# One core, one hybrid decoder layer: a hand-written order from the mixer's output projection to the first gate products of the MLP, split weights kept in DRAM, and 114-row transfers cut in two

## The chip, the core and the metric

The kernel runs on one core of a Trainium2 chip. The metric is the time on the device, in microseconds, of one execution; a kernel is run several times and the median counts. In what follows PE is TensorE (PEld its weight loads), ACT is ScalarE, DVE is VectorE, POOL is GpSimd and SP is SyncE, whose queue issues most of the DMAs.

## The reference

All data are float32; the layer is computed once (depth 1, batch 1, 1024 tokens of 1024 features, 16 learned tokens ahead of them).

```python
u = rmsnorm(h, mix_norm_pre[l])
q, f_logit, i_in, g_out, v_pool, gate_a, gate_b = jnp.split(u @ w_in[l], cuts, axis=-1)
a = hgrn2(q, f_logit, i_in, g_out, lbs[l], hgrn_out_norm[l])      # 4 heads, chunked recurrence
p = multiscale_pool(v_pool, pool_proj[l], pool_scale[l])          # trailing means, 4 groups
z = sigmoid(gate_a) * (a @ w_branch_hgrn[l]) + sigmoid(gate_b) * (p @ w_branch_pool[l])
h = h + rmsnorm(z @ w_out[l], mix_norm_post[l])
u = rmsnorm(h, ffn_norm_pre[l])
gt = causal_dwconv(u @ ffn_w_gate[l], ffn_conv_w[l], ffn_conv_b[l])     # 1024 -> 2816, width 3
y = (gelu(gt) * (u @ ffn_w_up[l])) @ ffn_w_down[l]
h = h + rmsnorm(y, ffn_norm_post[l])
```

The change concerns the sixth to the eighth of these lines: `z @ w_out`, the residual and the two norms, and the first products of `u @ ffn_w_gate`.

## The kernel before, in words

**Precision.** Every large product is made from three: both operands are split into a first part rounded to the matmul's format (`hi`, an ACT copy) and the rest (`lo`, a subtraction on DVE or POOL), and hi x hi, hi x lo and lo x hi are added up in PSUM (`mm3`, L158). For weights `wsplit` (L131) does this: a DMA on SP into `wraw` (three buffers), the ACT copy into `whi`, the subtraction into `wlo` (three buffers each). A `Loader` (L140) holds three weight blocks ahead: `ahead()` splits the block that comes three places later.

**The mixer's output.** 1026 tokens count here (the last two learned ones are kept for the convolution). They are taken in three thirds of 342 (`c`), each of three row tiles of 114 rows (`i`, RT = 114). `mix_mm` (L1055) runs over the eight feature blocks `k` of `w_out`; for each it takes the 128 x 1024 weight block, split in `whi` and `wlo`, and for each row tile and each half of the columns three matmuls: 18 per block, 144 per third, 432 in all. The split of `z` for a block (`split_z`, L935: an ACT copy, a DVE subtraction) is made four blocks ahead. The same 24 (c, k) weight blocks are loaded and split anew for each third; the subtraction runs on POOL, but for the last two blocks, which have it on DVE (L997).

**Behind each third.** `mix_out` (L1077) makes, for each row tile and half, the sum of squares (ACT) and the product with the gain into `m1` (DVE) out of PSUM. `vec` (L1090) takes the residual row (`load_res`, L1000, a load of 114 rows), finishes the norm, adds the residual, stores the sum `hs` to DRAM for the end of the kernel (L1096, a store of 114 rows), and norms the sum again into `un`. `feat` (L1099) transposes `un` on PE (L1017, eight transposes into one pair of PSUM banks) and fills the operands of the MLP, `to_quarters` (L1012). For a third, these steps are placed between the blocks of the next one (`reorder`, L1107, and the list at L1118).

**The MLP's products.** The gate and up projections use a Strassen scheme of seven products per pair of 128-column blocks (class `Strassen`, L180). Its moving operands are quarters of the activations: b11 and b21 are the two feature halves of the first 514 tokens, b22 the second feature half of the others, and t1 to t4 sums of quarters, which need all tokens. So P1 (b11) and P2 (b21) of the first four gate units can run before the last rows are normed: eight products of 24 matmuls. P6 (t2), P5 (t1), P3 (b22), P7 (t3) and P4 (t4) of the first unit follow. For a row tile behind token 512 `to_quarters` copies the transposes (ACT, `tt`), makes t1, t2, t3 and their hi and lo parts (DVE and ACT), the lo part of b22 and the difference for t4 (POOL); its last step, the parts of t4, is returned as a function (`t4s`) for later. `load_unit` (L220) loads a unit's weights and makes four weight sums on POOL. `ahead` (L199) of this class splits the weights of coming products, two products to a buffer, on DVE, but for products 5 to 8 of the early ones, which go to POOL (L210).

**What sets the order.** In most of the kernel a scheduler orders each engine's instructions by its own estimate, starting from program order; inside `tc.manual_schedule(engines=...)` the named engines keep program order. Before the change that holds for the start of the kernel and for POOL in the MLP (L1280), not for the mixer's output. SP is left to the scheduler in both kernels, and its queue issues in order: an issue that waits for a buffer holds back those behind it. Row tiles, z parts, `m1`, `un`, residual rows, t quarters and sums share 24 slots of SBUF (`slot`, L88); PSUM is four pairs of banks here (`pair`, L97), three of which a third of the mixer holds.

Of the kernel before, what the change touches and what calls it, by code (L numbers as in the profile page):

```python
# [8 lines left out]
F32 = mybir.dt.float32  # L9
# [47 lines left out]
def trunk_kernel(ctx: ExitStack, tc: tile.TileContext, x, meta_tokens, mix_norm_pre,  # L57
# [82 lines left out]
    class Loader:  # L140


        def __init__(self, srcs):
            self.srcs, self.got, self.at = srcs, [], 0
            self.ahead()

        def ahead(self):
            while len(self.got) < min(len(self.srcs), self.at + AHEAD):
                self.got.append(wsplit(*self.srcs[len(self.got)]))

        def next(self):
            self.at += 1
# [27 lines left out]
    class Strassen:  # L180
# [7 lines left out]
        def __init__(self, units, run, early, quarters, span, put, whole):  # L188
            self.units, self.run, self.early, self.bq = units, run, early, quarters
            self.span, self.put, self.whole = span, put, whole  # L190
            self.raws, self.sums, self.p1s, self.halves = {}, {}, {}, {}
            self.seq = []
            for e in range(0, early, 2):
                self.seq += [(e, "P1"), (e + 1, "P1"), (e, "P2"), (e + 1, "P2")]
            for u in run:
                self.seq += [(u, p) for p in self.ORDER if u >= early or p not in ("P1", "P2")]
            self.got, self.at = [], 0

        def ahead(self, n):  # L199

# [44 lines left out]
                return self.raws[u, "raw"][("P1", "P2", "P4").index(p)]  # L245
            return self.sums[u][("P5", "P6", "P7", "P3").index(p)]

        def product(self, u, p):

            assert self.seq[self.at] == (u, p)  # L250
            x = pair(p)
            self.at += 1
            whi, wlo = self.got[self.at - 1]
            q = self.MOVING[p]
            c0, o0, n = self.span(u)
            cuts = [(c0, o0, 512 - o0), (c0 + 512 - o0, 512, n - 512 + o0)][: 1 + (n + o0 > 512)]
            for k in range(4):
                xh, xl = (self.bq[q + h][k * len(self.bq[q + h]) // 4] for h in "hl")
                kk = k % xh.shape[1]
                xh, xl = xh[:, kk, :], xl[:, kk, :]  # L260
                for c, o, w in cuts:
                    pe.matmul(x[:, o : o + w], whi[:, k, :], xh[:, c : c + w], start=(k == 0), stop=False)  # L262
                    pe.matmul(x[:, o : o + w], whi[:, k, :], xl[:, c : c + w], start=False, stop=False)  # L263
                for c, o, w in cuts:
                    pe.matmul(x[:, o : o + w], wlo[:, k, :], xh[:, c : c + w], start=False, stop=(k == 3))  # L265
            self.ahead(4)
            return x[:, o0 : o0 + n]

        def half(self, key, i, n, name):

# [11 lines left out]
        def first(self, u):  # L282
            n = self.span(u)[2]
            key = (("e", u // 2), u % 2) if u < self.early else (("u", u), 0)
            self.p1s[u] = self.half(*key, n, "p1")
            return (lambda: act.copy(self.p1s[u], self.product(u, "P1")),
                    lambda: self.put(u, 0, 0, self.p1s[u], self.product(u, "P2")))

        def start_pair(self, e):
            p = [self.first(e + i) for i in range(2)]  # L290
# [697 lines left out]
    def add_quarters(*names):  # L988
        for q in names:
            for h in "hl":  # L990
# [3 lines left out]
    g3 = gain_bc(ffn_norm_pre, "g3")  # L994
    RT = CW // 3

    wo = Loader([(wblock(w_out[0], k, 1, 0, D), 1, D, dve if (c == 2 and k > 5) else pool_e)  # L997
                 for c in range(3) for k in range(KD)])

    def load_res(t0):  # L1000
        row = slot(D, name="row2")
# [1 line left out]
            nc.sync.dma_start(row[:HALO], meta_tokens[T0:NM, :])  # L1003
            nc.sync.dma_start(row[HALO:RT], x[0, 0 : RT - HALO, :])
        else:
            nc.sync.dma_start(row[:RT], x[0, t0 - HALO : t0 - HALO + RT, :])
        return row

    def t_tmp(n, name):
        return slot(n, name=nm(name))  # L1010
# [41 lines left out]
        pool_e.tensor_tensor(dst, rr(fq[q + "h"][0][:, :, d]), src, ALU.subtract)  # L1052
        pool_e.tensor_tensor(dst, rr(fq[q + "l"][0][:, :, d]), dst, ALU.add)

    def mix_mm(c, between, zs):  # L1055
        rows.update({c * CW + i * RT: load_res(c * CW + i * RT) for i in range(3)})
        banks = [pair_banks("pm") for _ in range(3)]
        znext = []
        for k in range(KD):
            whi, wlo = wo.next()  # L1060
            if k == KD - 1 and c < 2:
                znext = [split_z(c + 1, k_) for k_ in range(ZA)]
            zh, zl = zs[k]
            for i in range(3):
                t = slice(i * RT, (i + 1) * RT)
                for j in range(2):
                    n = slice(j * 512, (j + 1) * 512)
                    mm3(banks[i][j][:RT], (zh[:, t], zl[:, t]), (whi[:, 0, n], wlo[:, 0, n]), k == 0, k == KD - 1)
            wo.ahead()
            if k + ZA < KD:  # L1070
                zs.append(split_z(c, k + ZA))
            if between:
                for f in between.pop(0):
                    f()
        return banks, znext

    def mix_out(c, banks, g2, g3):  # L1077
        todo = []
        for i in range(3):
            m1 = slot(D, name="m1")  # L1080
            ssq = small([P, 2], "ssq2", "mq", 6)
            for j in range(2):
                n = slice(j * 512, (j + 1) * 512)
                junk = t_tmp(512, "junk")
                act.activation(junk[:RT], banks[i][j][:RT], AF.Square, accum_out=ssq[:RT, j : j + 1])
                dve.tensor_tensor(m1[:RT, n], banks[i][j][:RT], g2[:RT, n], ALU.mult)  # L1086
            un = {}
            t0 = c * CW + i * RT

            def vec(i=i, m1=m1, ssq=ssq, un=un, t0=t0):  # L1090
                row = rows.pop(t0)
                s = small([P, 1], "mss", "ms")
                dve.tensor_tensor(s[:RT], ssq[:RT, 0:1], ssq[:RT, 1:2], ALU.add)
                rstd = row_rstd(s, RT, "m")
                dve.scalar_tensor_tensor(m1[:RT], m1[:RT], rstd[:RT], row[:RT], ALU.mult, ALU.add)
                nc.sync.dma_start(hs[t0 : t0 + RT, :], m1[:RT])  # L1096
                un[0] = norm_rows(m1, RT, g3)

            def feat(un=un, t0=t0):  # L1099
                return to_quarters(un[0], t0, pair_banks())  # L1100

            todo += [vec, feat]
        return todo

    rows = {}

    def reorder(t):  # L1107

        v0, f0, v1, f1, v2, f2 = t
        return [[v0], [v1], [f0], [v2], [f1], [f2]]  # L1110

    between = []
    for c in range(2):
        banks, z0 = mix_mm(c, between, z0)
        between = reorder(mix_out(c, banks, g2, g3))
    v0, v1_, f0, v2_, f1, f2 = (x_[0] for x_ in between)
    t4s = []
    banks, _ = mix_mm(2, [[v0], [v1_, v2_], [f0], [lambda: add_quarters("t2", "t3", "t4"), lambda: t4s.append(f1())],  # L1118
                          [lambda: t4s.append(f2())], [lambda: [f() for f in t4s]]], z0)


    WD = ffn_w_down[0]
# [31 lines left out]
    def add_later(all_=False):  # L1154
        tick[0] += 1
        for e in [e for e in later if all_ or e[0] <= tick[0]]:
            later.remove(e)
            pool_e.dma_start(e[1], e[2], accum_op=ALU.add)

    v0, f0, v1_, f1, v2_, f2 = mix_out(2, banks, g2, g3)  # L1160

    UNITS = ([(j, 0) for j in range(EARLY)] + [(j, 1) for j in range(EARLY)]
             + [(j, up) for j in range(EARLY, KF // 2) for up in range(2)])
# [97 lines left out]
        return [((yh[:, h], yl[:, h]), (wh[:, h], wl[:, h])) for h in (slice(0, 512), slice(512, 1024))]  # L1261


    ffn.begin()
    v0()
    v1_()
    v2_()
    t4s = []
    for e in range(0, EARLY, 2):
        p = ffn.start_pair(e)  # L1270
        p[0][0]()
        p[1][0]()
        t4s.append((f0 if e == 0 else f2)())
        p[0][1]()
        if e == 0:
            t4s.append(f1())
        p[1][1]()
    for f in t4s:
        f()
    with tc.manual_schedule(engines={E.Pool}):  # L1280
        ffn.finish()
        add_later(True)
# [146 lines left out]
```

## Time and profile before

| | |
|---|---|
| median of 3 runs | 1434.69 us (1431.66 to 1434.87) |
| the profiled execution's own time | 1431.93 us |
| its span, first to last instruction | 1430.1 us |
| mean granted TensorE clock | 0.979 |
| busy PE / DVE / ACT / POOL | 95% / 68% / 40% / 40% of the span |
| the mixer's output, first to last matmul | 605.6 to 728.1 us |

How to read it: the profile is one execution. Times are from the span's start. Busy shares are means over stages with different limits, so the stage from 605 to about 800 us is read by itself, in windows. An instruction that waits for a port or a lock counts as busy; matmuls overlap, and their rate is read from the distance of their starts. The granted clock is the share of the full TensorE clock. Where a row ends in `[4.33 <-DVE m L1086]`, the engine was idle for 4.33 us before the instruction and that one released it. The DMA share is the mean busy share of the core's 16 DMA engines.

### The profile page before, as it was taken

How to read it: one execution, taken by the hardware profiler on the slowest of the kernel's cores; microseconds unless marked ns; L12 is line 12 of the kernel's file. 1: busy time of each engine (PE TensorE's matmuls, PEld its weight loads, DVE VectorE, ACT ScalarE, POOL GpSimd, SP SyncE). 2: the span in 40 equal slices, each digit the busy share in tenths (PEclk: the TensorE clock that was granted, in tenths of full speed). 3: DMA queues.
4: the chain of work that ended last, by engine and by line, in shares of the span. 5: the costliest groups of instructions: out<-in, count | busy, mean ns of one | idle time of the engine just before them, and what ended most of it. 6: DMA issues, size and time to landing. Idle time of an engine off the chain costs nothing. (4 is left out here: it accounts for less than half of the span.)

```text
span 1430.1 us, 21631 instructions
## 1 busy us (share of the span) xinstructions
PE 1364.1 (95%) x8405; PEld 1233.2 (86%) x8405; DVE 976.1 (68%) x1406; ACT 570.1 (40%) x981; POOL 570.3 (40%) x400
## 2 busy tenths in 40 slices
PE   8989999999999999998968999999999999999976
PEld 6789999999999899976658888888899998888765
DVE  6784545489876754625678888888888775445476
ACT  6443333366654452244464322322222233333353
POOL 4255421237354410253348565544556642001051
PEclk9999999999999999999988999999999999999998
DMA  6034333321110033644542577666677798565546
GB/s 240 36 97 141 126 111 104 97 60 45 33 47 5 23 133 103 218 139 153 166 126 80 142 232 206 186 174 158 162 166 165 169 259 232 194 194 180 191 158 218
DMA packets 129562, 202.65 MB, mean 142 GB/s; under 512 B 7739, under 2 KB 75935, under 8 KB 129460
## 3 DMA queue, kind: packets, MB, share of 16 engines
q1 hardware_dynamic: 118548, 181.08, 37.9%
q0 software_dynamic: 10912, 20.19, 9.4%
q8 instruction: 66, 1.08, 0.3%
q14 instruction: 36, 0.29, 0.1%
HBM read 152.45 MB, written 71.85 MB: 157 GB/s over the span
## 5 line engine op out<-in xcount | busy, mean ns | idle before, releaser
L137 POOL TENSOR_TENSOR wlo<-wraw,whi 128x1024 fp32r<-128x1024 f32 (+2 forms) x37 | 85.3, 2311 | 228.2 <-ACT whi L136 146.5
L262 PE MATMUL P<-v,whi 128*128 128x258 f32 (+2 forms) x528 | 165.8, 328 | 10.9 <-DVE m L1086 4.3
L263 PE MATMUL P<-v,whi 128*128 128x258 f32 (+2 forms) x528 | 164.8, 325 | 0.7 <-POOL v L327 0.7
L265 PE MATMUL P<-v,wlo 128*128 128x258 f32 (+2 forms) x528 | 143.0, 325 | 0.0
L161 PE MATMUL pd<-rot 128*128 128x512 f32 x284 | 111.9, 394 | 8.6 <-DVE rot L1249 8.6
L262 PEld LDWEIGHTS P<-v,whi 128*128 128x128 f32 x528 | 103.1, 195 | 19.1 <-DVE m L1086 4.5
L136 ACT CAST whi<-wraw 128x1024 fp32r<-128x1024 f32 (+2 forms) x60 | 52.9, 884 | 158.6 <-PE pba L174 26.7
L162 PE MATMUL pd<-rot 128*128 128x512 f32 x284 | 111.3, 392 | 0.0
L263 PEld LDWEIGHTS P<-v,whi 128*128 128x128 f32 x528 | 103.1, 195 | 8.8 <-POOL v L327 1.0
L1249 DVE TENSOR_TENSOR rot<-yt,rot 128x1024 fp32r<-128x1024 f32 (+1 forms) x38 | 46.8, 1231 | 90.1 <-ACT rot L1248 90.1
L209 ACT CAST whi<-wraw 128x512 fp32r<-128x512 f32 x90 | 53.2, 617 | 109.6 <-PE P L263 94.4
L265 PEld LDWEIGHTS P<-v,wlo 128*128 128x128 f32 x528 | 90.0, 194 | 7.8
L1133 POOL TENSOR_TENSOR ys<-y 128x512 f32<-128x512 f32 x22 | 34.3, 1559 | 142.0 <-issue 99.4
L210 DVE TENSOR_TENSOR wlo<-wraw,whi 128x512 fp32r<-128x512 f32 x82 | 73.7, 921 | 18.2 <-ACT whi L209 18.2
L235 POOL TENSOR_TENSOR swa<-wraw,wraw 128x512 f32<-128x512 f32 x30 | 47.4, 1582 | 95.5 <-DMA wraw<-in_w_in_dram 62.3
L1248 ACT CAST rot<-yt 128x1024 fp32r<-128x1024 f32 (+1 forms) x38 | 37.7, 995 | 118.7 <-PE pd L161 118.7
L160 PE MATMUL pd<-rot 128*128 128x512 f32 x284 | 75.8, 390 | 1.2 <-ACT rot L1248 1.2
L161 PEld LDWEIGHTS pd<-rot 128*128 128x128 f32 x284 | 53.8, 190 | 21.5 <-DVE rot L1249 10.3
L209 ACT CAST whi<-swa 128x512 fp32r<-128x512 f32 x60 | 35.8, 618 | 87.8 <-PE P L263 74.9
L1183 DVE SCALAR_TENSOR_TENSOR y<-g,par,y 128x1024 f32<-128x1024 f32 x44 | 64.1, 1457 | 0.7
L160 PEld LDWEIGHTS pd<-rot 128*128 128x128 f32 x284 | 53.2, 188 | 12.7 <-ACT rot L1248 1.6
L162 PEld LDWEIGHTS pd<-rot 128*128 128x128 f32 x284 | 53.8, 190 | 11.2
(347 smaller groups left out, 4306.9 us busy)
## 6 DMA issues: line engine op xcount, KB each, us to landing
wraw<-in_w_in_dram SPq DMA_DIRECT2D x36, 512.0 KB, 3.5
yt<-ysum SPq DMA_DIRECT2D x33, 512.0 KB, 3.6
wraw<-in_ffn_w_gate_dram SPq DMA_DIRECT2D x26, 512.0 KB, 8.3
wraw<-in_w_out_dram SPq DMA_DIRECT2D x24, 512.0 KB, 8.7
wraw<-in_ffn_w_up_dram SPq DMA_DIRECT2D x22, 512.0 KB, 4.7
wsum<-in_ffn_w_down_dram SPq DMA_DIRECT2D x22, 512.0 KB, 5.9
ysum<-ys SPq DMA_DIRECT2D x11, 768.0 KB, 4.6
sa<-sscr SPq DMA_DIRECT2D x16, 513.0 KB, 5.2
```

The lines of the kernel that those rows point to most:

```text
L136: act.copy(hi, raw)
L137: eng.tensor_tensor(lo, raw, rr(hi), ALU.subtract)
L160: pe.matmul(ps, ahi, bhi, start=first, stop=False)
L161: pe.matmul(ps, ahi, blo, start=False, stop=False)
L162: pe.matmul(ps, alo, bhi, start=False, stop=last)
L209: act.copy(hi, src)
L210: (pool_e if 4 <= i < 2 * self.early else dve).tensor_tensor(lo, src, rr(hi), ALU.subtract)
L235: pool_e.tensor_tensor(s1, a21, a22, ALU.add)
L262: pe.matmul(x[:, o : o + w], whi[:, k, :], xh[:, c : c + w], start=(k == 0), stop=False)
L263: pe.matmul(x[:, o : o + w], whi[:, k, :], xl[:, c : c + w], start=False, stop=False)
L265: pe.matmul(x[:, o : o + w], wlo[:, k, :], xh[:, c : c + w], start=False, stop=(k == 3))
L1183: dve.scalar_tensor_tensor(a, g[:, :, j : j + n], cvw[:, j, m : m + 1], a, ALU.mult, ALU.add)
```

## The change

The stage from the mixer's output to the first gate products is written anew.

1. *Second parts kept.* In the first third, each `lo` part of `w_out` is also stored to DRAM by a DMA that POOL issues. In the other two thirds it is loaded from there, into the `wlo` buffer itself, instead of being subtracted again.
2. *Transfers.* The residual loads and the `hs` stores of 114 rows become one of 112 rows and one of 2.
3. *Order.* `mix_mm`, `mix_out` and `reorder` go. PE, ACT, DVE and POOL keep program order from the first matmul of the mixer's output to the last part of t4. A third's squares, gain products and adds come at its end; its norms and transposes come in the next third, the transposes behind blocks 2, 3 and 4. The last three blocks of the last third run row tile by row tile, and each tile's steps start when it is complete. Squares and gain products are one instruction per row tile of 1024 columns, no longer two of 512.
4. *Early products.* A product can have a consumer (`then`) that is placed ahead of the next weight splits, and the number of splits ahead is listed by hand (`prompt`). The transposes of the last third come after the third, fourth and sixth of the eight early products.

```diff
+    wlos = [dram.tile([P, D], F32, name=f"wlos{k}") for k in range(KD)]
+
+    def wo_parts(c, k):
+        if c == 0:
+            hi, lo = wsplit(wblock(w_out[0], k, 1, 0, D), 1, D, pool_e)
+            pool_e.dma_start(wlos[k], rr(lo[:, 0]))
+            return hi, lo
+        raw = wraw_tile()
+        nc.sync.dma_start(raw, w_out[0][k * P : (k + 1) * P])
+        hi, lo = (wst.tile([P, D], F32R, tag=t, name=nm(t)) for t in ("whi", "wlo"))
+        nc.sync.dma_start(rr(lo), wlos[k])
+        act.copy(hi, raw)
+        return [t.rearrange("p (k c) -> p k c", k=1) for t in (hi, lo)]
...
+    def by_rows(move):
+        for r in (slice(0, RT - HALO), slice(RT - HALO, RT)):
+            move(r)
...
-            nc.sync.dma_start(row[:RT], x[0, t0 - HALO : t0 - HALO + RT, :])
+            by_rows(lambda r: nc.sync.dma_start(row[r], x[0, t0 - HALO + r.start : t0 - HALO + r.stop, :]))
...
+        def take(self, i):
+            m1, ssq = slot(D, name="m1"), small([P, 1], "ssq2", "mq", 6)
+            junk = t_tmp(D, "junk")
+            act.activation(junk[:RT], self.x[i][:RT], AF.Square, accum_out=ssq[:RT])
+            dve.tensor_tensor(m1[:RT], self.x[i][:RT], g2[:RT], ALU.mult)
...
+        def add(self, i):
+            rstd = row_rstd(self.ssq[i], RT, "m")
+            dve.scalar_tensor_tensor(m1[:RT], m1[:RT], rstd[:RT], rows.pop(t0)[:RT], ALU.mult, ALU.add)
+            by_rows(lambda r: nc.sync.dma_start(hs[t0 + r.start : t0 + r.stop, :], m1[r]))
+        def norm(self, i):
+            act.activation(un[:RT], m1[:RT], AF.Square, accum_out=ssq[:RT])
+            rstd = row_rstd(ssq, RT, "n")
+            dve.scalar_tensor_tensor(un[:RT], m1[:RT], rstd[:RT], g3[:RT], ALU.mult, ALU.mult)
...
+    with tc.manual_schedule(engines={E.PE, E.Activation, E.DVE, E.Pool}):
+        for c in range(3):
+            tiles_ = [pair("pm") for _ in range(3)]
+            own = Rows(c, tiles_)
+            for k in range(KD if c < 2 else KD - 3):
+                w = wo.next()
+                for i in range(3):
+                    mix_tile(c, k, w, tiles_[i], i)
+                if k == KD - 1:
+                    for i in range(3):
+                        own.take(i)
+                wo.ahead()
+                next_z(1)
+                if k == 0 and c > 0:
+                    load_rows(c)
+                if last:
+                    if k < 2:
+                        last.norm(k + 1)
+                    if k in (2, 3, 4):
+                        if c == 2 and k == 3:
+                            add_quarters("t2", "t3", "t4")
+                        t4s.append(last.feat(k - 2))
+                    if k > 4 and t4s:
+                        t4s.pop(0)()
+            if c < 2:
+                own.add(0)
+                own.add(1)
+                own.norm(0)
+                own.add(2)
+                last = own
+        ffn.load_first(0)
+        ffn.load_first(1)
+        ffn.load_first(2)
+        ws = [wo.next() for _ in range(3)]
+        for i in range(3):
+            for k in range(KD - 3, KD):
+                mix_tile(2, k, ws[k - KD + 3], tiles_[i], i)
+            own.take(i)
+            if i == 0:
+                own.add(0)
+                t4s.pop(0)
+                t4s.pop(0)()
+            if i == 1:
+                ffn.ahead(2)
+                own.norm(0)
+                own.add(1)
+        ffn.ahead(4)
+        ffn.load_first(3)
+        ffn.prompt = [5, 6, 8, 8, 8, 10, 10, 11]
+        p = [ffn.first(e) for e in range(EARLY)]
+        p[0][0]()
+        own.norm(1)
+        own.add(2)
+        p[1][0]()
+        own.norm(2)
+        p[0][1]()
+        ffn.load_unit(RUN[0])
+        t4s.append(own.feat(0))
+        p[1][1]()
+        t4s.append(own.feat(1))
+        p[2][0]()
+        p[3][0]()
+        t4s.append(own.feat(2))
+        p[2][1]()
+        p[3][1]()
+        for f in t4s:
+            f()
     with tc.manual_schedule(engines={E.Pool}):
         ffn.finish()
```

`mix_tile` is the inner loop of `mix_mm` for one row tile, `next_z(1)` the next `split_z`, `load_rows` the three residual loads of a third, and `feat` calls `to_quarters` as before.

More of the change, by code (lines that the diff above doesn't have):

```diff
@@ L265, in product @@
                     pe.matmul(x[:, o : o + w], wlo[:, k, :], xh[:, c : c + w], start=False, stop=(k == 3))
+            x = x[:, o0 : o0 + n]
+            if then and self.prompt:
+                then(x)
+                self.ahead(self.prompt.pop(0) - self.at)
+                return x
             self.ahead(4)
-            return x[:, o0 : o0 + n]
+            if then:
+                then(x)
+            return x
         def half(self, key, i, n, name):
@@ L1077, in mix_out @@
[L1077 to L1119, printed above, removed]
+    rows, z_at = {}, {}
```

74 lines of the change are left out of this document (32 added, 42 removed).

## The prediction

> **What bounds the kernel now.** I read the page first, for the engine that is full and for the slices in which it isn't, and then the stage that the change touches, by windows. The page says that TensorE sets the time nearly everywhere; the dips of its row and of PEclk lie in its 19th to 22nd slice, which are 643 to 787 us (a slice is 1430.1 / 40 = 35.75 us).
>
> ```profile
> span 1430.1 us, 21631 instructions
> PE 1364.1 (95%) x8405; PEld 1233.2 (86%) x8405; DVE 976.1 (68%) x1406; ACT 570.1 (40%) x981; POOL 570.3 (40%) x400
> PE   8989999999999999998968999999999999999976
> PEclk9999999999999999999988999999999999999998
> ```
>
> The windows below are the first third of the mixer output, its second and last third, the eight early gate products with the three last row tiles, and what follows until TensorE runs without a gap again (from 801.5 us). The columns are length, busy time and instructions of PE, PEld, DVE, ACT and POOL, then the granted clock, the DMA share and GB/s.
>
> ```profile
> 605.50:640.00 34.50, 34.50 (x151) 26.32 (x150) 10.82 (x15) 13.06 (x21) 19.20 (x8) 1.00 0.45 148
> 640.00:685.00 45.00, 38.87 (x166) 29.20 (x166) 25.32 (x36) 22.65 (x48) 19.88 (x8) 0.92 0.48 156
> 685.00:728.50 43.50, 39.22 (x170) 29.37 (x169) 31.97 (x48) 20.55 (x47) 13.74 (x6) 0.92 0.47 150
> 728.50:768.70 40.20, 30.32 (x216) 29.84 (x216) 35.08 (x56) 24.42 (x63) 25.69 (x19) 0.83 0.38 125
> 768.70:801.50 32.80, 24.69 (x146) 22.34 (x145) 26.63 (x26) 10.56 (x21) 31.24 (x25) 0.84 0.22 49
> ```
>
> A window loses its idle PE time, and (1 - clock) of its length, because the granted clock is full or half and follows the gaps. That is 0 in the first third; 6.1 + 3.6 = 9.7 us in the second; 4.3 + 3.5 = 7.8 in the last; 9.9 + 6.8 = 16.7 in the early products; 8.1 + 5.2 = 13.3 after them. In all 47.5 us (an upper bound: some half-clock time is idle anyway), and no rearrangement here can gain more.
>
> Who made TensorE wait in the two thirds? The waits of 640 to 730 us (total, times, longest) and three stretches of DMA:
>
> ```profile
> POOL wlo L137 <- ACT whi L136: 35.0, 7, 13.6
> ACT whi L136 <- DMA wraw<-in_w_out_dram: 11.5, 4, 8.3
> ACT zc L938 <- DMA hscr<-m: 9.5, 1, 9.5
> PE pt L1017 <- DVE un L345: 5.3, 3, 2.2
> ```
> ```profile
> 664.00:672.00 8.00, 5.09 (x24) 4.03 (x23) 1.48 (x3) 1.29 (x3) 0.00 (x0) 0.88 0.38 157
> 709.00:717.00 8.00, 8.00 (x41) 6.23 (x40) 0.33 (x1) 0.01 (x1) 0.00 (x0) 1.00 0.38 156
> 602.00:604.00 2.00, 2.00 (x15) 2.00 (x14) 2.00 (x1) 0.00 (x0) 1.19 (x1) 1.00 1.05 399
> ```
> ```profile
> wraw<-in_w_out_dram SPq DMA_DIRECT2D x8, 512.0 KB, 3.1
> wraw<-in_w_out_dram SPq DMA_DIRECT2D x4, 512.0 KB, 20.3
> ```
>
> The DMA share stands at 0.38 for 8 us twice, right behind the residual loads and hs stores. 0.38 is 6 of 16 engines: six are full and ten have nothing. The same machine moved 399 GB/s at 602 us. The 114-row transfers run on six engines, the weight blocks have a share on those six, and so their landing goes from 3.1 us (605 to 640) to 20.3 us (640 to 672). ACT waits for them, POOL waits for ACT, and TensorE last. The 9.5 us are the same thing: a slot that an hs store holds until it has landed. The second cause is DVE: the normed rows come late for the transposes.
>
> **The change part by part.**
>
> *The split 112 + 2.* Eight loads and nine stores become two transfers each. On 16 engines, 112 rows take 157/399 of the time, and the backlog goes. Seventeen more issues on SP at about 0.3 us each (below) are hidden: 5 us, spread over more than 100. What is late next in the two thirds is the un chain.
>
> *The second parts in DRAM.* Of 24 subtractions of w_out, 16 go: 14 on POOL, 2 on DVE. Prices, and what the others do to DVE:
>
> ```profile
> 657.27 2.40 POOL L137 TENSOR_TENSOR wlo<-wraw,whi 128x1024 fp32r<-128x1024 f32 x1 [2.75 <-ACT whi L136]
> 800.84 0.80 POOL L1158 DMA_DIRECT2D wsum<-wsum  x1
> ```
> ```profile
> 657.60 2.44 DVE L939 TENSOR_TENSOR zc<-sa,zc 128x342 fp32r<-128x342 f32 x1 [0.16 <-ACT zc L938]
> 661.89 0.51 DVE L939 TENSOR_TENSOR zc<-sa,zc 128x342 fp32r<-128x342 f32 x1
> ```
> ```profile
> 643.80 0.29 SPq L1096 DMA_DIRECT2D hscr<-m  x1
> 644.18 0.33 SPq L133 DMA_DIRECT2D wraw<-in_w_out_dram  x1
> ```
>
> The same zc subtraction takes 0.51 us alone and 2.44 beside a POOL subtraction, which it waits out: the two engines take turns on operands in SBUF. So 14 x 2.40 = 33.6 us of POOL go and with them DVE's waiting. Added: 8 stores from POOL in the first third, 0.8 to 1.6 us each by the L1158 row (256 KB; these are 512). Beside the 2.40 that is at most 4.0 us per block of 18 matmuls, and a block takes 18 x 0.233 = 4.19 us (spacing in the rows below), so nothing waits. Added too: 16 loads of 512 KB. Two blocks' time, 8.4 us, lies between the release of a wlo buffer and its next use, against 3.1 us of landing for one block and some 4.4 for two behind each other (512 KB at 399 GB/s are 1.3). Cost taken 0; above, it is a rival.
>
> ```profile
> 605.56 0.39 PE L160 MATMUL pm<-whi,zc 128*114 128x512 f32 x1
> 605.79 0.39 PE L161 MATMUL pm<-wlo,zc 128*114 128x512 f32 x1
> ```
>
> *The hand order in the thirds.* Transposes of a third come at k = 2, 3, 4 of the next, after 12.6 us; one full-width row operation takes 1.28 us (below), and three m1, three add and two un on DVE, 8 x 1.3 = 10.4 us, are through by then. PSUM: the fourth pair takes tile 0 of the next third at once. I leave 2 us for small waits: 17.5 becomes 2, a gain of 15.5 (10 to 17.5).
>
> *The hand order behind them.* The last three blocks run tile by tile, so take, add and norm of the first tile move ahead of the end, and the t-sums of the third before, too. New waits: ACT holds P1's operand copies until the third tile has used a weight buffer (6 matmuls, 1.4 us, into it; norm(0) and the last take are queued behind, no product waits: 0 to 1.5 us, taken 0). Feature transposes move behind one more product. Residual rows are now asked for one block into a third; their adds come seven blocks later, so that costs 0. The first gate weights are asked for five blocks into the last third, in buffers that are free by then, behind the last w_out loads on SP: 0. What TensorE waited for before:
>
> ```profile
> 735.68 0.58 PE L262 MATMUL P<-v,whi 128*128 128x258 f32 x1 [4.33 <-DVE m L1086]
> 746.75 0.99 PE L1017 MATMUL pt<-ident,un 114*128 114x114 f32 x4 [5.56 <-DVE un L345]
> 773.50 0.55 PE L262 MATMUL P<-v,whi 128*128 128x258 f32 x1 [4.13 <-DVE g L1191]
> 791.71 0.49 PE L262 MATMUL P<-v,whi 128*128 128x512 f32 x1 [2.44 <-DVE g L1193]
> ```
>
> The first two go: ahead of un of tile 1, DVE has an add, the last m1, two lo parts and un itself, 1.3 + 1.3 + 1.4 + 1.3 = 5.3 us by the prices below, some 7 with the ACT steps between; its transposes come behind four products, some 12 us (half of the 23.5 below). Next is P6, which needs t2 of all three tiles; eight products and the transposes are 40.2 - 16.7 = 23.5 us of TensorE. Prices of what DVE and POOL must do by then:
>
> ```profile
> 648.21 1.28 DVE L1095 SCALAR_TENSOR_TENSOR m<-m,rstd,row 114x1024 f32<-114x1024 f32 x1
> 763.50 0.69 DVE L327 TENSOR_TENSOR t2l<-tt,t2h 128x228 fp32r<-128x228 f32 x2
> 764.12 0.68 DVE L210 TENSOR_TENSOR wlo<-swa,whi 128x512 fp32r<-128x512 f32 x1
> 764.72 0.62 DVE L1035 TENSOR_TENSOR tt<-tt,tt 128x456 f32<-128x456 f32 x1
> ```
> ```profile
> 733.41 2.73 POOL L210 TENSOR_TENSOR wlo<-wraw,whi 128x512 fp32r<-128x512 f32 x2 [0.64 <-ACT whi L209]
> 736.10 0.99 POOL L1052 TENSOR_TENSOR tt<-v,tt 128x456 f32<-128x456 f32 x1
> 764.27 5.61 POOL L1052 TENSOR_TENSOR tt<-v,tt 128x456 f32<-128x456 f32 x1 [2.34 <-DVE t2l L327]
> 820.23 1.30 POOL L235 TENSOR_TENSOR swa<-wraw,wraw 128x512 f32<-128x512 f32 x1
> ```
>
> DVE: two add and two un, 5.1; four lo parts, 2.7; a tile's quarters 5 x 0.62 + 2 x 0.69 = 4.5, two of them 9.0; the third as far as t2, 2.5: 19.3 us. POOL: four lo parts 5.5, four weight sums 5.2, three operations on each of two tiles 6.0: 16.7. One after another this is 36 us, and P6 waits 12.5; if DVE always goes first, it is covered by the 23.5. Both are seen: the POOL operation of 0.99 us that stretches to 5.61 let eight DVE operations by, and the 2.44 above is the contrary. I take the middle, 7 us of waiting, and 2 of half clock behind it: 16.7 becomes 9 to 9.5, a gain of 7.5. The Trainium skill (SBUF — State Buffer, section "SBUF: two separate sides") calls the shared port an exclusive lock that whoever starts first holds for the whole instruction. By that the 36 us would hold, a rival below; the trace agrees on the lock (2.44 against 0.51), not on a fixed turn.
>
> Behind P6 the t4 parts and next weight sums stay, on the same two engines. The 2.44 us is theirs and stays; the 4.13 should shrink. I take half of 13.3 as gained, 7 (0 to 13).
>
> Sum: 15.5 + 7.5 + 7 = 30 us. From the profiled execution's 1431.9 us: 1401.9. That execution lies 2.8 us under the median of the runs, 1434.7, so against it 1404.7; I say 1404.
>
> **The rivals.** (a) *The lock keeps the tail.* P6 waits its 12.5 and 2 of clock, and nothing is gained behind it: 15.5 + 2.2 = 18 us, 1417. For it: in the last two windows the busy times of DVE and POOL make 60.8 us in 40.2 and 57.9 in 32.8, so that for much of it one counts as busy while it waits for the other. Against: 33.6 us of POOL are gone ahead of it.
>
> (b) *The tail is smooth as well*: 15.5 + 15 + 11 = 41.5, 1393. For it: most of its waits are chains from late rows. Against: the 36 us.
>
> (c) *The weights come too late: slower.* The thirds now move 16 x 1.05 MB and 12 row transfers of 0.47 MB, 1.4 MB per block, by one queue in order; a wlo load can't start before its buffer is free. At 157 GB/s a block takes 8.9 us, 16 take 143 instead of 88.5; with the tail's 14.5 gained the end is 1434.7 + 54 - 14.5 = 1474. It decides from 6.4 us per block, 217 GB/s, on ((88.5 + 14.5)/16). For it: the thirds' windows show only 150 to 156 GB/s. Against: that is six engines and demand; 399 was seen, 334 is wanted.
>
> (d) *The split does not spread.* If the 112 rows stay on six engines, the 0.38 plateaus stay, and of the thirds only DVE's relief is left, 4 us: 18.5 in all, 1416. No row isolates a 112-row transfer. The Trainium skill (DMA: Bandwidth & Descriptors, "Rules for kernel authors") says not to bother with two transfers to disjoint partition halves, since they serialize; that would be this rival. The same page ("Why a DMA increments its semaphore by 16 and not by 1") picks the largest engine count up to 16 that divides the rows: 6 for 114, 16 for 112; the trace agrees with the 6 (0.38).
>
> **How the numbers follow.** Forecast 0.48, (a) 0.22, (b) 0.12, (c) 0.08, (d) 0.05; 0.05 for gains and new waits that cancel out (0.04 within 0.3%, 0.01 beyond). The range runs from (b) less 3 us, 1390, to (a) and (d) with 8 us more of waiting in the thirds, 1425; (c) is left out. 0.3%, 4.3 us, is about what a measurement of this kernel can tell: faster 0.87, same 0.04, slower 0.09.
>
> **What would show it.** Right: no 0.38 plateau between 640 and 730 us, wraw landing under 6 us, no POOL wlo after the first third, TensorE idle under 3 us there, the last mixer matmul near 713 us, P6 about 31 us later with a wait for DVE. Wrong: ACT whi or PE waiting for DMA wlo (c); the plateau still there (d); P6 waiting over 10 us (a) or under 2 (b); new gaps behind the seam, where the load is unchanged.

## The result: 22.6 us less, and the profile after

The median after is 1412.18 us (1411.57 to 1414.52, 4 runs) against 1434.78 us before (1431.66 to 1434.91, 4 runs): a ratio of 0.9851, 95% interval 0.9833 to 0.9869. The forecast was 1404 us, in a range of 1390 to 1425.

The profiled execution after took 1414.52 us, the slowest of its four, and the profiled one before 1431.93, near the fastest of its own. So the two spans differ by less than the medians, by 17.4 us. After's mixer output also starts 2.6 us later (608.2 against 605.6 us), behind work that the change does not touch; from that start to the end of the span it is 824.5 before and 804.5 after, 20.0 us.

From the page of after: the four lines that stand in the prediction for before.

```profile
span 1412.7 us, 21638 instructions
...
PE 1357.2 (96%) x8405; PEld 1226.8 (87%) x8405; DVE 973.9 (69%) x1377; ACT 569.1 (40%) x963; POOL 530.8 (38%) x394
...
PE   8989999999999999999987999999999999999976
...
PEclk9999999999999999999998999999999999999998
```

The dip that ran over four slices is two slices wide now. POOL lost 39.5 us of busy time and DVE 2.2. Below are two windows in the second and the last third, where before had its stretches at a DMA share of 0.38; then the same five stages as in the prediction, from the first mixer matmul to the end of the gaps; then the last two of them once more, with another border between them:

```profile
660.00:670.00 10.00, 8.16 (x39) 6.05 (x39) 3.49 (x6) 4.81 (x8) 0.00 (x0) 1.00 0.98 382
692.00:702.00 10.00, 9.40 (x51) 7.26 (x49) 2.87 (x6) 4.08 (x7) 0.00 (x0) 1.00 1.03 361
```
```profile
608.20:642.70 34.50, 34.50 (x151) 26.28 (x150) 20.07 (x13) 13.92 (x21) 17.84 (x12) 1.00 0.90 302
642.70:680.20 37.50, 35.66 (x167) 27.20 (x166) 19.12 (x30) 22.84 (x42) 0.00 (x0) 1.00 0.85 298
680.20:717.50 37.30, 35.82 (x166) 26.93 (x165) 26.84 (x45) 23.72 (x54) 6.48 (x8) 1.00 0.72 246
717.50:757.10 39.60, 29.05 (x221) 27.96 (x220) 35.45 (x42) 20.02 (x46) 20.00 (x14) 0.91 0.40 129
757.10:789.90 32.80, 29.33 (x163) 25.47 (x164) 28.83 (x31) 13.62 (x28) 25.47 (x22) 0.90 0.32 64
```
```profile
717.50:753.70 36.20, 28.42 (x218) 27.55 (x218) 32.57 (x38) 19.62 (x44) 20.00 (x14) 0.91 0.43 141
753.70:789.90 36.20, 29.95 (x169) 25.88 (x168) 31.72 (x36) 14.02 (x29) 25.47 (x22) 0.91 0.29 58
```

Read as in the prediction (idle PE time, plus one minus the clock times the length), these are the us that each stage loses:

| | thirds 2, 3 | early products | behind them | sum |
|---|---|---|---|---|
| before | 9.7 + 7.8 | 16.7 | 13.3 | 47.5 |
| forecast | 2 | 9.2 | 6.3 | 17.5 |
| after, border behind P6's wait (757.1) | 1.8 + 1.5 | 14.1 | 6.8 | 24.2 |
| after, border behind the last early product (753.7) | 1.8 + 1.5 | 11.0 | 9.5 | 23.8 |

The thirds came as forecast. For the two stages behind them the border matters. The stage before ended with the last early product, at 768.7 us, and its wait of 4.13 us in P6 and the products mixed with it lay behind that. The forecast's 9.2 holds P6's wait, and so does the window of after that ends at 757.1. By this border the early products kept nearly all of their loss; by the border of before they lose 11.0 us. Only the two together compare: 30.0 us before, 15.5 forecast, 20.9 after. The five longest waits of TensorE from 717.5 to 790 us:

```profile
719.25 0.50 PE L265 MATMUL P<-v,wlo 128*128 128x258 f32 x2 [1.07 <-DVE wlo L210]
743.93 1.78 PE L1043 MATMUL pt<-ident,un 114*128 114x114 f32 x8 [5.17 <-DVE g L1197]
757.14 0.38 PE L262 MATMUL P<-t2h,whi 128*128 128x256 f32 x1 [2.81 <-ACT t2h L333]
774.72 0.47 PE L262 MATMUL P<-v,whi 128*128 128x512 f32 x1 [0.96 <-DVE p L308]
785.83 0.68 PE L262 MATMUL P<-v,whi 128*128 128x512 f32 x1 [1.75 <-DVE g L1197]
```

The two waits for late rows (m1 4.33, un 5.56 us) are gone, as forecast. A new one is as long: the third tile's transposes need a pair of PSUM banks, and the pair is held until DVE has made a gate sum (`g`, L1197). In DVE's order that sum stands behind the first tile's quarters, and these were slow. DVE's rows, then POOL's at the same time:

```profile
737.17 1.73 DVE L1063 TENSOR_TENSOR tt<-tt 128x456 f32<-128x456 f32 x1
738.83 1.69 DVE L334 TENSOR_TENSOR v<-tt,v 128x456 fp32r<-128x456 f32 x1
740.45 2.82 DVE L334 TENSOR_TENSOR t3l<-tt,t3h 128x228 fp32r<-128x228 f32 x2
743.20 0.68 DVE L1197 TENSOR_TENSOR g<-p,P 128x514 f32<-128x514 f32 x1
...
748.86 0.62 DVE L1063 TENSOR_TENSOR tt<-tt 128x456 f32<-128x456 f32 x1
749.40 0.63 DVE L334 TENSOR_TENSOR v<-tt,v 128x456 fp32r<-128x456 f32 x1
```
```profile
736.94 1.48 POOL L235 TENSOR_TENSOR swa<-wraw,wraw 128x512 f32<-128x512 f32 x1 [2.06 <-DMA wraw<-in_ffn_w_gate_dram]
738.50 1.54 POOL L236 TENSOR_TENSOR swa<-swa,wraw 128x512 f32<-128x512 f32 x1
740.00 1.65 POOL L237 TENSOR_TENSOR swb<-wraw 128x512 f32<-128x512 f32 x1
741.61 1.41 POOL L238 TENSOR_TENSOR swb<-wraw,swa 128x512 f32<-128x512 f32 x1
```

The same two operations take 0.62 and 0.63 us for the second tile, before POOL's next operation starts and as it does (749.51), and 1.73 and 1.69 beside POOL's weight sums. Four DVE operations and four POOL operations went by in turns, in 6.0 us.

### The profile page after: what moved, and what is told of

The parts are those of the page before. It is cut to its first block, busy times and chain, and to the rows that moved or that the text cites. A ratio compares the mean times of both kernels' runs of the same rounds, so it can differ in the third digit from the quotient of the medians.

```text
span 1412.7 us, 21638 instructions
## 1 busy us (share of the span) xinstructions
PE 1357.2 (96%) x8405; PEld 1226.8 (87%) x8405; DVE 973.9 (69%) x1377; ACT 569.1 (40%) x963; POOL 530.8 (38%) x394
## 3 DMA queue, kind: packets, MB, share of 16 engines
q0 software_dynamic: 12064, 24.38, 10.3%
## 5 line engine op out<-in xcount | busy, mean ns | idle before, releaser
L262 PE MATMUL P<-v,whi 128*128 128x258 f32 (+2 forms) x528 | 162.9, 323 | 4.2 <-DVE g L1197 2.4
L263 PE MATMUL P<-v,whi 128*128 128x258 f32 (+2 forms) x528 | 162.1, 321 | 0.0
L137 POOL TENSOR_TENSOR wlo<-wraw,whi 128x1024 fp32r<-128x1024 f32 (+2 forms) x23 | 50.1, 2176 | 183.2 <-ACT whi L136 101.5
L262 PEld LDWEIGHTS P<-v,whi 128*128 128x128 f32 x528 | 100.8, 191 | 12.9 <-DVE g L1197 2.8
L263 PEld LDWEIGHTS P<-v,whi 128*128 128x128 f32 x528 | 100.9, 191 | 7.7
L136 ACT CAST whi<-wraw 128x1024 fp32r<-128x1024 f32 (+2 forms) x44 | 36.2, 825 | 146.3 <-PE pba L174 31.3
L161 PEld LDWEIGHTS pd<-rot 128*128 128x128 f32 x284 | 53.8, 189 | 21.5 <-DVE rot L1255 10.3
L160 PEld LDWEIGHTS pd<-rot 128*128 128x128 f32 x284 | 53.2, 188 | 12.7 <-ACT rot L1254 1.6
L210 DVE TENSOR_TENSOR wlo<-swb,whi 128x512 fp32r<-128x512 f32 x60 | 55.9, 937 | 12.0 <-ACT whi L209 11.8
```

Source lines behind the costliest of these rows:

```text
L137: eng.tensor_tensor(lo, raw, rr(hi), ALU.subtract)
L160: pe.matmul(ps, ahi, bhi, start=first, stop=False)
L161: pe.matmul(ps, ahi, blo, start=False, stop=False)
L210: (pool_e if 4 <= i < 2 * self.early else dve).tensor_tensor(lo, src, rr(hi), ALU.subtract)
```

## The experiments

Theory: the cut into 112 + 2 rows made the thirds' gain, and POOL's work beside DVE is what kept the tail. Rivals: the gain belongs to the order by hand or to the kept parts; the tail is limited by the place of its steps in the queues, not by the two engines' sharing. Ratios are against the kernel before, run on the same chip.

**The cut alone: e1_split_only** is the kernel before with only this:

```diff
+    def by_rows(move):
+        for r in (slice(0, RT - HALO), slice(RT - HALO, RT)):
+            move(r)
...
-            nc.sync.dma_start(row[:RT], x[0, t0 - HALO : t0 - HALO + RT, :])
+            by_rows(lambda r: nc.sync.dma_start(row[r], x[0, t0 - HALO + r.start : t0 - HALO + r.stop, :]))
...
-                nc.sync.dma_start(hs[t0 : t0 + RT, :], m1[:RT])
+                by_rows(lambda r: nc.sync.dma_start(hs[t0 + r.start : t0 + r.stop, :], m1[r]))
```

> The kernel before, with only its 114-row loads and stores cut into 112 and 2. Theory A (the six-engine backlog is the main wait of the two later thirds): the thirds lose most of their 18 us of excess, the 0.38 plateaus go, landing of wraw falls under 6 us; time 1434.8 - 11 = 1424, 1420 to 1427. Rival B (the thirds wait for DVE beside POOL's subtractions, the transfers are late without being the cause): 1430 to 1435. Rival C (112 rows stay on six engines): no change in time, plateaus stay.

1416.34 us, 0.9886 (0.9872 to 0.9899), below theory A's 1420 to 1427. A stretch of its second third, then its last four stages, as above:

```profile
649.00:657.00 8.00, 7.84 (x40) 5.81 (x39) 7.50 (x5) 5.61 (x12) 8.00 (x3) 1.00 0.97 277
```
```profile
640.10:677.10 37.00, 34.97 (x165) 26.60 (x164) 26.97 (x36) 22.55 (x47) 20.91 (x8) 1.00 0.61 190
677.10:714.10 37.00, 35.73 (x169) 27.39 (x168) 33.35 (x49) 22.77 (x53) 15.40 (x9) 1.00 0.56 174
714.10:754.10 40.00, 30.38 (x222) 29.43 (x220) 36.48 (x53) 24.14 (x61) 21.90 (x18) 0.87 0.39 128
754.10:787.10 33.00, 26.00 (x157) 23.61 (x158) 30.42 (x34) 11.47 (x22) 29.23 (x22) 0.90 0.23 49
```

Where the cut transfers run, the share is 0.97, and no backlog stays behind on six engines. The stages lose 2.0 + 1.3, 14.8 and 10.3 us: the two stages behind the thirds gained as well (25.1 for 30.0), and theory A had left that out. The thirds are as good as in the kernel after, with POOL still subtracting and no order by hand; the rest of the change is worth the 4.2 us that stand in the two later windows (28.4 against 24.2).

**The cut taken out: e2_no_split** is the kernel after with whole transfers (`by_rows` calls `move(slice(0, RT))`).

> The changed kernel with its transfers of 114 rows whole again. Theory A: six engines carry 5.6 MB of rows and 6/16 of 16.8 MB of weights in the thirds, 11.9 MB at 157 GB/s, 76 us for 73 us of matmuls, with waits at each seam: the thirds grow by 8 to 15 us, time 1420 to 1428. Rival B: the hand order gives the transfers time enough, 1412 to 1415.

1440.54 us, 1.0049 (1.0035 to 1.0062): slower than before, and beyond both expectations. Its waits in the second and last third (total, times, longest), and one stretch in windows:

```profile
ACT whi L1016 <- DMA wraw<-in_w_out_dram: 31.6, 2, 16.6
...
PE pm L161 <- DMA wlo<-wlos: 26.7, 5, 12.6
```
```profile
660.00:670.00 10.00, 1.21 (x9) 0.92 (x9) 0.63 (x1) 0.25 (x1) 0.00 (x0) 0.66 0.82 206
```

This is rival (c), the weights that come too late: 206 GB/s in this stretch, where 217 was its break-even. What the kept parts have to do with the loss, e4 shows.

**The kept parts taken out: e3_no_keep** is the kernel after with the subtraction in all thirds (`wo_parts` returns `wsplit(...)` on POOL, the last two blocks on DVE, as before).

> The changed kernel with the second parts of w_out subtracted in all three thirds again (POOL, the last two blocks on DVE), nothing kept in DRAM. Theory A' (DVE and POOL take turns, and 16 subtractions cost the thirds and the seam): thirds 3 to 6 us longer by late zc and un parts, tail 1 to 2 us longer: 1416 to 1420. Rival (the loads of kept parts press the DMA engines as much as the subtractions press POOL): 1410 to 1414, with the waits for DMA wlo gone.

1421.75 us, 0.9927 (0.9914 to 0.9939), just above theory A'. Two windows (the second and the last third), then one wait of the second:

```profile
642.80:685.80 43.00, 37.52 (x167) 28.96 (x166) 33.55 (x29) 22.79 (x42) 20.20 (x8) 0.92 0.48 161
685.80:728.90 43.10, 37.66 (x167) 28.93 (x166) 38.53 (x49) 25.26 (x57) 17.13 (x12) 0.92 0.48 155
```
```profile
664.76 1.75 PE L1033 MATMUL pt<-ident,un 114*128 114x114 f32 x8 [5.48 <-DVE v L334]
```

Each third loses 8.9 us: transposes fixed behind blocks 2, 3 and 4 meet a DVE that is busy for 33.6 and 38.5 us of 43, beside POOL's subtractions.

**Neither: e4_order_only**, the kernel after with both edits undone, so that the order by hand is left.

> The changed kernel with both undone: 114-row transfers whole, second parts subtracted in all thirds; the hand order alone. If the parts add up: the thirds keep most of the excess of before (10 to 15 us of 18), the tail its gain of 6: 1420 to 1428. If the hand order is most of the gain: 1412 to 1417. If a strict order suffers more from late transfers than the scheduler's: over 1430.

1446.48 us, 1.0094 (1.008 to 1.0108): the order alone costs 14 us, the last of its three expectations. e2 differs from it only by the kept parts. So with whole transfers, too, these gain 6 us under the order by hand, late as they come, and the loss in e2 comes with the order. With the cut they gain 11 (after against e3, by the ratios).

**The cut and the kept parts, without the order: e5_split_keep** is e1_split_only with `wo_parts` and `wlos`.

> The kernel before with the cut transfers and with the kept second parts, in the scheduler's order: the whole change but the hand order. Theory H (the kept parts pay only under the hand order, which without them was 11.5 us longer in the thirds): the thirds had only some 4 us of excess left with the cut transfers alone, so 1412 to 1417, near the 1416.3 of the cut alone. Rival (the hand order is worth nothing at all): 1410 to 1413, no slower than the whole change. If the kept parts' loads crowd the queue under the scheduler: 1418 to 1425.

1421.31 us, 0.992 (0.9908 to 0.9933), 5 us slower than the cut alone. So with the cut, the order alone (e3) and the kept parts alone (e5) each cost 5 us, and both together gain 4 to 5. For e3 the rows say why; for e5 they say only where (TensorE waits 3.2 us for kept parts in the thirds, and its first wait in the early products for `m1` is 5.50 us, 2.99 with the cut alone); what makes the latter longer stays open.

**Another place for the quarters: e6_put_first** is the kernel after with the first tile's quarters behind the next product's step, so that the gate sum comes ahead of them on DVE. `trans` makes the transposes and copies them out of PSUM, and returns the rest of `to_quarters` as a function:

```diff
...
-        t4s.append(own.feat(0))
+        r0 = own.trans(0)
         p[1][1]()
-        t4s.append(own.feat(1))
+        r1 = own.trans(1)
+        t4s.append(r0())
+        t4s.append(r1())
```

> The changed kernel with the quarter operations of row tile 0 behind the second gate sum on DVE (its evacuation of a PSUM pair first), and the copies out of the transposes' pair at once. Theory L (DVE and POOL together have some 36 us of work ahead of P6, whatever the order): the 5.2 us wait of the third transposes goes, and the wait at P6 grows by nearly as much: 1410 to 1413. Rival P (the strict order holds a PSUM pair, and that is the loss): wait and half clock go, 5 to 8 us: 1404 to 1407.

1412.47 us, 0.986 (0.9847 to 0.9874): no change. The wait for the gate sum is gone and a longer one stands ten us further on:

```profile
753.42 0.58 PE L262 MATMUL P<-v,whi 128*128 128x258 f32 x1 [8.93 <-ACT p L293]
```

**POOL's difference later: e7_diff_late** is the kernel after with `negdiff` moved into the returned function, so that POOL makes the t4 differences after everything that P6 needs:

```diff
-        negdiff(t2, t2, "b21", d)
-        return lambda: put("t4", t2, d, pool_e)
+        def t4():
+            negdiff(t2, t2, "b21", d)
+            put("t4", t2, d, pool_e)
+        return t4
```

> The changed kernel with the two POOL differences for t4 of each row tile moved into the t4 step at the end, so that POOL has 2 x 1.1 us less per tile beside DVE's quarters. Theory L: P6 comes 3 to 4 us earlier, of which the end keeps some: 1408 to 1411, and a new wait before P4 of up to 2 us. Rival P (order and PSUM pairs, not the shared turns): 1411 to 1414, or later if P4 waits.

1417.12 us, 0.9887 (0.9874 to 0.9901): slower, where 1408 to 1411 was expected. The wait ahead of P6 shrank to 1.62 us, and P4, which needs t4, now waits 8.83 where it waited 0.24:

```profile
774.70 0.58 PE L262 MATMUL P<-t4h,whi 128*128 128x258 f32 x1 [8.83 <-ACT t4h L333]
```

The mechanism was as the theory had it, but the work was only moved, and the size of the new wait was missed.

**POOL's sums on DVE: e8_sums_dve** is the kernel after with the first unit's four weight sums on DVE, behind the first two tiles' quarters (`sums = ffn.load_unit(RUN[0], True)`, later `sums(dve)`).

> The changed kernel with the first unit's four weight sums on DVE behind row tile 1's quarters, no longer on POOL beside row tile 0's. DVE has 2.7 us more, POOL 6.1 us less. Theory L: row tile 0's quarters take about 5 us and not 10.6, the gate sum behind them comes 5 us earlier, the third transposes wait 0 to 1 us, P6 comes about 3 us earlier: 1408 to 1411. Rival (DVE alone is the bound, POOL gives way): P6 2.7 us later, 1413 to 1416.

1410.27 us, 0.9833 (0.9819 to 0.9846). A sum takes 0.69 us on DVE for 1.41 to 1.65 on POOL, and the third transposes wait 3.00 us, no longer 5.17 (0 to 1 was expected):

```profile
748.50 0.69 DVE L239 TENSOR_TENSOR swa<-swa,wraw 128x512 f32<-128x512 f32 x1
```
```profile
740.36 1.00 PE L1049 MATMUL pt<-ident,un 114*128 114x114 f32 x8 [3.00 <-DVE g L1203]
```

**The suspected cost doubled: e9_sums_twice** makes the same four sums on POOL two times over.

```diff
-            pool_e.tensor_tensor(s1, a21, a22, ALU.add)
...
+            for _ in range(2 if u == self.run[0] else 1):
+                pool_e.tensor_tensor(s1, a21, a22, ALU.add)
...
```

> The kernel after, with POOL's four weight sums of the first unit (L235 to L238) made twice over, so that one suspected cost is doubled; nothing else differs. In the kernel after these four run from 736.9 to 743.0 us, beside the first tile's quarters on DVE, which take 10.6 us there and 4.5 by their uncontended rows. Theory L (DVE and POOL take turns, and their sum decides the tail): 6 us more of POOL hold DVE for 3 to 6 us more, P6 starts that much later, and the time is 1415 to 1418 us. Theory Q (POOL's work only fills its gaps; what counts is the order on DVE): POOL stands idle for some 8 us between its steps from 747 to 758 us, the added sums use those, P6 stays, and the time is 1411.5 to 1413.5.

1415.9 us, 0.9895 (0.9879 to 0.991). The eight sums run from 740.34 to 752.7 us, and behind the wait for the gate sum TensorE has a second one:

```profile
747.33 1.78 PE L1044 MATMUL pt<-ident,un 114*128 114x114 f32 x8 [5.24 <-DVE g L1198]
756.98 0.39 PE L263 MATMUL P<-v,whi 128*128 128x258 f32 x1 [4.35 <-ACT p L294]
```

In the kernel after, the second of these was 0.88 us. Against e10, which was measured in the same rounds and does in this stage what the kernel after does, 6 us more of POOL cost 3.9 us. It would have been nothing if POOL's work only filled its gaps.

**More transfers: e10_more_dma** adds a copy of 512 KB from DRAM to spare DRAM behind each load of a kept part.

> The kernel after, with one more DMA of 512 KB behind each kept part in the second and last third: it copies the weight block from DRAM to spare DRAM, which nobody reads. The queue then has 1.9 MB per block of 4.19 us. Theory M (the loads of the thirds are near the limit of the DMA engines; 399 GB/s was seen): a block takes at least 1.9 MB / 399 GB/s = 4.8 us, 16 blocks 9 us more, TensorE waits for wlo and ACT for wraw, and the two thirds take 85 us or more instead of 76: 1420 us or more. Rival S (the small waits for wlo come from latency, not from the rate, and there is room): the thirds stay within 2 us of 76, and the time is 1411 to 1415.

1412.03 us, 0.9851 (0.9837 to 0.9865), and it leaves the question open: the copies depend on nothing, and the scheduler, to which SP is left, issued all sixteen at the start of the kernel.

```profile
L1017 SPq DMA_DIRECT2D spare<-in_w_out_dram x16: 488/536/2094, 21.9 to 40.4; - x16
```

How near the thirds' loads are to costing time was therefore not measured. It serves as a second measurement of the kernel after.

**More taken from POOL: e11_all_dve** is e8 with the lo parts of the early products 5 to 8 and of b22 on DVE as well.

> The kernel with the first unit's sums on DVE (which took 1410.3 us), with two more steps taken from POOL to DVE: the lo parts of the early products 5 to 8 (on POOL 1.3 to 2.1 us each, on DVE 0.7) and the lo parts of b22 (on POOL 1.3 to 1.5 us, on DVE 0.7). POOL keeps the difference and the parts of t4. Theory L (turns, the sum of both decides): the sum of DVE and POOL falls by some 6 us, half of it ahead of P6: 1405 to 1409 us. Rival V (DVE alone is now the bound of the tail): DVE has 5 us more in front of P6, which eats it: 1410 to 1414.

1409.35 us, 0.9846 (0.983 to 0.9861). The third transposes' wait is down to 0.65 us, but others for `g`, `p`, `whi`, `tt` and `t2h` stand behind it, 0.90 to 2.68 us each. From the first early product to P6 TensorE's waits add up to 10.6 us, as many as in the kernel after. Against e10 it is 2.7 us, with intervals that overlap: between the two expectations.

**The tail left to the scheduler: e12_tail_sched** has the order by hand for the thirds only; the statements from the last three blocks to the last t4 part stand as they are, outside `manual_schedule`.

> The kernel after, with the order by hand only for the thirds: from the last three blocks of the last third on, through the early products and the last transposes, the engines are left to the scheduler again, from the same program order. Theory H (the order by hand is what lets the early products follow the last third at once; without it the early products ended 10 us later): 1416 to 1420 us. Rival (the scheduler does as well, once the steps stand in this program order and POOL has less to do; the order matters in the thirds alone): 1410 to 1414.

1409.18 us, 0.9844 (0.9829 to 0.9858), 2.9 us under e10, again with overlapping intervals. The order by hand of the tail brings nothing that these runs can tell: the rival held, a little below its own range.

e8, e11 and e12 have the lowest medians, but none is clearly faster than the kernel after.

## Why the prediction was right, and where its size was off

**The thirds: right.** 15.5 us were forecast and 14.2 came. The reason given, six engines of 16 for 114 rows, is shown by e1: the one edit lets the transfers run at a share of 0.97 and takes the loss from 17.5 to 3.3 us. Rival (d) falls with that. The Trainium skill (DMA: Bandwidth & Descriptors, "Rules for kernel authors") says not to bother with transfers to disjoint halves; here two transfers on disjoint rows gained 16 us over one, because, as the same page's divisor rule has it ("Why a DMA increments its semaphore by 16 and not by 1"), 112 rows divide by 16 and 114 only by 6. What the prediction credited beside the cut, 33.6 us of POOL and DVE's relief, was not needed for it in the scheduler's order: e1 still has POOL's subtractions, with DVE waiting beside them, and loses the same 3.3. Under the order by hand it was: e3 loses 17.8. Of the signs named for this part the plateau is gone (shares of 0.98 and 1.03 above); TensorE idles 3.3 us in the two thirds, where under 3 was named; the time that a weight block takes to land is not in the trace of after.

**The loads: right by a small margin.** Rival (c) was refused because 399 GB/s had been seen. The windows of after show 382 and 361 GB/s at a share of 0.98 and 1.03, ACT waits for weight blocks and TensorE for kept parts, but for little (total, times, longest, in the two thirds):

```profile
ACT whi L1016 <- DMA wraw<-in_w_out_dram: 9.5, 2, 4.8
...
PE pm L161 <- DMA wlo<-wlos: 1.5, 2, 0.9
```

In e6 and e9, whose thirds are the same, TensorE has single waits of 2.63 and 2.54 us for a kept part.

**The early products: the step that failed.** "I take the middle, 7 us of waiting, and 2 of half clock": a loss of about 9.2 up to P6, and 14.1 was measured. The middle was taken between turns of DVE and POOL (36 us of work) and "DVE always goes first" (19.3), without a row that would place it there. Both bounds were too low, because the list of DVE's work ahead of P6 was short. From 717.5 to 757.1 us the kernel after has on DVE, among others:

```profile
L1120 DVE SCALAR_TENSOR_TENSOR un<-m,rstd,g 114x1024 f32<-114x1024 f32 x3 | 3.9, 1286 | 0.1
L1106 DVE TENSOR_TENSOR m<-pm,g 114x1024 f32<-114x1024 f32 x2 | 2.4, 1214 | 0.0
L1197 DVE TENSOR_TENSOR g<-p,P 128x514 f32<-128x514 f32 x2 | 1.4, 680 | 0.0
```

The prediction's sum has two `un`, no gain product into `m1` and no gate sum, and four lo parts of weights where there are seven. With these and the small reciprocals it is about 27 us, an estimate by the prices without POOL beside them. By its own working, P6 would then wait 20 us by turns and 3.5 with DVE first; the middle is 12, and TensorE was idle for 10.6.

What POOL's work costs DVE is seen from the last mixer matmul to the end of P6's wait, in after, e9, e7 and e11:

```profile
717.32:757.14 39.82, 29.23 (x223) 28.14 (x221) 35.66 (x44) 20.05 (x46) 20.00 (x14) 0.91 0.40 128
720.51:764.35 43.84, 30.17 (x223) 29.09 (x221) 39.45 (x44) 20.15 (x46) 25.96 (x18) 0.92 0.36 116
716.27:752.78 36.51, 29.67 (x222) 28.80 (x221) 31.63 (x43) 19.84 (x46) 15.12 (x10) 0.91 0.43 140
715.47:754.01 38.54, 27.97 (x222) 26.26 (x220) 35.01 (x54) 20.54 (x47) 5.50 (x4) 0.98 0.38 122
```

With 6.0 us more of POOL the stretch is 4.0 us longer, with 4.9 us less it is 3.3 shorter: here about two thirds of POOL's time was added to DVE's. That is rival (a)'s mechanism in part, and the gain by the same border, 2.6 us, is close to its 2.2. But e11 has 14.5 us less of POOL and some 6.7 more on DVE, and is only 1.3 us shorter, with DVE busy for 35.0 of 38.5 us. So DVE's own work, which the sum had too small, holds P6 back as well, and moving POOL's work to DVE brings little. How the missing 5 us divide between the short list and the sharing, the runs do not separate.

The prediction had also put the whole wait at P6. It was split: 5.17 us at the third transposes, through a PSUM pair that DVE had to free, and 2.81 at P6, with half clock behind both. e6 says that this place of the steps is not what costs: without the wait at the transposes the same stretch takes 40.6 us. The last mixer matmul starts at 717.3 us, not 713 (2.6 of it from the later start), and P6 goes on 40 us behind it, not 31:

```profile
717.32 0.40 PE L162 MATMUL pm<-whi,zc 128*114 128x512 f32 x1
```

**Behind P6: near, but half of 13.3 was a guess.** By the border behind P6's wait 6.5 us came for 7, where (a) had 0; by the border of before 3.8 came, and 5.7 in the early products. Nothing in the prediction derives the half, so the hit is luck in part. What the two stages gained together, 9.1 us for 14.5, does not depend on the border by more than half a microsecond. So the result, 1412, lies between the forecast and (a)'s 1417, nearer to (a).

The windows give 14.2 + 2.6 + 6.5 = 23.3 us, with half clock counted in full; the spans gave 20.0 from the stage's start, the medians 22.6.

**The parts do not add up singly.** The prediction summed them as if they did. The order by hand is a loss of 14 us without the cut, and without the kept parts it gives back 5 of what the cut brings. The kept parts gain 6 us and 11 under the order by hand, without and with the cut, and cost 5 in the scheduler's order with it. They land in time only with the cut, and the order needs them to have DVE free.

## What to carry to other kernels

Look at the DMA share for flat stretches: 0.38 was 6 of 16 engines, and splitting the transfer so that its larger part has a row count with a large divisor (112 is 7 x 16) was worth more than all the reordering. When DVE and POOL both read operands in SBUF in a stretch that is late, list all that the first of them does, and add a good part of the other's work: here all of DVE's and about two thirds of POOL's. Take work away rather than move it to another place. An order written by hand is worth something only if its steps are ready where it puts them, and a kept result gained under one order and cost time under another: test such edits together and apart.

## What the runs showed of the hardware

A DVE operation of 0.62 us and a POOL operation of 1.30 (the prediction's row of a weight sum) that run in turns take 1.5 us a pair: four pairs in 6.0 us, less than their sum, 1.9, and more than the longer one. DVE's instruction is the one stretched, to 1.4 to 1.7; POOL's only to between 1.41 and 1.65. The Trainium skill (SBUF — State Buffer, "SBUF: two separate sides") has the port pair locked for a whole instruction; the turns agree, the pair's 1.5 us is less than a full lock would give.

A copy from DRAM to DRAM of sixteen times 512 KB at 22 to 40 us cost no time that can be measured (1412.03 against 1412.18 us; both have the ratio 0.9851 to before).
